# Two layers of a hybrid decoder on one core: recurrence outputs kept token-major, the forget gate inside a keys group, column groups interleaved in pairs

## The chip, the cores and the metric

The kernel runs on one core of a Trainium2 chip, as one launch. The metric is device time in microseconds (us), lower is better. Beside the timed runs there is one profiled execution, whose span is counted from its first to its last instruction. The engines are named as in the profile: PE is TensorE (matrix products), PEld its weight loads, DVE is VectorE, ACT is ScalarE, POOL is GpSimd, SP is SyncE, which here only issues DMAs.

## The reference, cut to what matters

256 tokens of width 2048 go through two layers. Every layer is a mixer and a gated MLP, each behind an RMS norm and added to the residual.

```python
# layer 0: mixer A (gMLP) and mixer B (HGRN2), 8 heads of 128 each
u, v, q, f, i, g = split(h @ w_in)
y_a = gelu(u) * (causal(sp_w) @ rms(gelu(v)) + sp_b)
k = (1 - lb) * sigmoid(-f);  decay = lb + (1 - lb) * sigmoid(f)
# state_t = decay_t * state_(t-1) + k_t v_t;  o_t = q_t state_t  (v is i here)
y_b = rms(o) * o_gain * silu(g)
x = x + concat(y_a, y_b) @ w_out
# layer 1: forgetting attention, 16 heads of 128
q, k, v, g, f = split(h @ w_in)           # f: 16 columns, one per head
c = cumsum(log_sigmoid(f + b_f))
p = softmax(rms(q) @ rms(k).T * scale + c[t] - c[s], causal)
x = x + ((p @ v) * sigmoid(g)) @ w_out
# both layers
z = conv3(h @ w_up);  x = x + (silu(z_a) * z_b) @ w_down
```

All weights and activations are float32.

## The kernel before, in words

The residual x lies feature-major, as 16 tiles of 128 features by 256 tokens (`xT`). A projection is made in groups of 512 output columns. Every float32 weight tile `w` comes from HBM by SP (L164), ACT rounds it to `wh` (L173), DVE subtracts to get the rest `wl` (L176), and PE sums three products of 128x512 for each of 16 k tiles and each of two token halves: high by high, high by low, low by high. That is 96 products in a group (`project_tok` L230 to L232; `project_four` L247 to L249, whose weights are four blocks of 128 columns). A step of the k loop brings two k tiles, so one `w` is 128x1024, half a megabyte; there are four buffers of `w` and three each of `wh` and `wl`, and six and five where `deep["pool"]` adds a second pool. The sums stand in PSUM banks of the pool `pm` (four banks, two for a group); everything small uses the four banks of `px`.

The group's result is token-major (tokens on partitions). Where the next step wants it feature-major, `transposed` (L252) turns it: two DVE block transposes (L255), then 16 DMAs of 32 KB, half of them issued by SP and half by POOL (L261).

Everything beside the main products is written as generators. `tick()` (L122), called once in every k step, admits generators from `queue` to `flight` up to `depth` and moves each on by one `yield`; so the position of a side step in program order is set by counting ticks. `LAG` ticks pass between the turning DMAs and their consumers, `WAIT` before the norm is finished. The framework then orders each engine's instructions by that program order and by its own estimate of when an instruction is ready; an order between two instructions can be added by hand (`add_manual_dep`).

Layer 0's mixer: two groups for v, then twice (j = 0, 1) the groups f, q, i of four heads, then two groups g, two groups u, four groups of the output projection (L707). The first group of the kernel is fed while x arrives (`feed`, `single`): its weights come in halves of 256 KB. For each head of mixer B, `hgrn` (L560) works feature-major on the tile `kq` with the second 128 tokens stored backwards: products of q and k on PE of which only the diagonal is kept (L568, L569), seven levels of masked scores (L599), a last cross product (L603), three products with the values `itok` (L620 to L622), whose second half was reversed before by a product with a permutation matrix (L662), a norm over the head, and two PE transposes (L635) back to feature-major with the gain (L638). `gated` (L672) multiplies that by silu(g) turned to feature-major, and `split` makes the high and low parts for the output projection, which takes mixer B's eight k tiles first (`names=ks`).

Layer 1's mixer: the first q group and the first k group (`early`, L723), `norm.finish()` (L726, a product L359 and a norm over tokens), the forget gate as a product group of its own (`forget` L734, through `project` L197 and L200: weights of 128 columns of which 16 count, result feature-major), then v and the other groups. q and k are normed and turned; `columns` (L751) transposes the summed gate; `attend` (L760) handles one head; `gate` (L843) multiplies by sigmoid(g) and turns; four groups of output projection.

The MLP (`ffn`, L881): `up` makes one group for each half of the gate, turns them (`tmp` has one buffer, `zt` two), convolves and multiplies; `down` sums over the hidden tiles. Groups run one after another everywhere: all 16 k tiles of one, then all 16 of the next.

Of the kernel before, what the change touches and what calls it, by code (L numbers as in the profile page):

```python
# [25 lines left out]
LAG = 4  # L26
WAIT = 4
EPS = 1e-6
WARM = 8
# [22 lines left out]
def tile_trunk(ctx: ExitStack, tc: tile.TileContext, x, pp_d, cst_d, mlev_d, msk_d,  # L52
# [30 lines left out]
    first_dma = nc.sync.dma_start(pp[:, 0:C_FFN], pp_d[:, 0:C_FFN])  # L83
# [24 lines left out]
    def back(ap):  # L108
        return view(ap, P - 1, (-1, P))

# [9 lines left out]
    flight, queue = [], []  # L120

    def tick():  # L122
        while queue and len(flight) < depth[0]:
            flight.append(queue.pop(0))
        for g in list(flight):
            if next(g, flight) is flight:
                flight.remove(g)
# [3 lines left out]
    def start(g):  # L131

        if next(g, g) is not g:
            flight.append(g)
# [5 lines left out]
    def drain():  # L140
        while flight or queue:
            tick()

    deep = {"pool": None, "turn": 0, "dma": first_dma}

    def in_order(r):
        tc.add_manual_dep(r.ins, deep["dma"].ins.name, order, reason="queue order")
        deep["dma"] = r


    def weights(src, n, rows=None, single=None):
# [17 lines left out]
        for i, p in enumerate(parts):  # L169
            if single:  # L170
                norm, k = single
                norm.feed_split(k + i, SC if k + i else V)
            deep["act"] = SC.activation(wh[:, p], w[:, p], AF.Copy)  # L173
            if deep["turn"] == 5:
                deep["hold"] = deep["act"]
            V.tensor_tensor(wl[:, p], w[:, p], wh[:, p].bitcast(F32), ALU.subtract)  # L176
        return wh, wl

    def project(wsrc, acts, chunks=(8, 8), k0=0, run=2, narrow=False):
# [3 lines left out]
        for c in chunks:  # L183
# [3 lines left out]
            for k1 in range(0, c, run):  # L187
# [11 lines left out]
                for k in ks:  # L199
                    PE.matmul(ps[:, S:2 * S], wl[:, k * P:(k + 1) * P], acts[done + k][:, 0:S],  # L200
                              start=False, stop=done + k == nk - 1, skip_group_check=True)
# [3 lines left out]
    def project_tok(wsrc, norm, feed=False):  # L205
        ps = [pm.tile([P, 512], F32, tag="pm", name=nm("pm")) for _ in range(2)]
        k = 0
        for c in (2,) * 8:
            if feed and k >= 8:
                for i in range(c):  # L210
                    norm.feed_split(k + i)
            tick()
            wh, wl = weights(wsrc[:, k * 512:(k + c) * 512], c * 512, single=(norm, k) if feed and k < 8 else None)
            if feed and k in BEHIND:
                in_order(nc.sync.dma_start(*fetch[BEHIND[k]]))
            if feed and k < 8:
                for i in range(c):
                    a = norm.a[k + i]
                    for j, (o, t) in enumerate(((0, wh), (S, wh), (0, wl))):
                        for T in range(2):  # L220
                            PE.matmul(ps[T], a[:, o + T * P:o + (T + 1) * P], t[:, i * 512:(i + 1) * 512],  # L221
# [3 lines left out]
            for T in range(2):  # L225
                for i in range(c):
# [5 lines left out]
                    PE.matmul(ps[T], al, h, start=False, stop=k + i == KT - 1)  # L232
# [3 lines left out]
    def project_four(w4, acts, n, k0=0, names=None):  # L236
        ps = [pm.tile([P, 512], F32, tag="pm", name=nm("pm")) for _ in range(2)]
        for k in range(0, n, 2):
            tick()
            lo = (k0 + k) * P  # L240
            wh, wl = weights(w4[:, :, lo:lo + 2 * P].rearrange("m p c -> p m c"), 1024, 4)
            for T in range(2):
                for i in range(2):
                    a = acts[names[k + i] if names else k + i]
# [4 lines left out]
                    deep['mm'] = PE.matmul(ps[T], al, h, start=False, stop=k + i == n - 1)  # L249
        return ps  # L250

# [13 lines left out]
    def fold(ps):  # L265
        t = tp.tile([P, S], F32, tag="ev", name=nm("ev"), bufs=3)
        SC.activation(t, ps[:, S:2 * S], AF.Copy)
        V.tensor_tensor(t, ps[:, 0:S], t, ALU.add)
        return t

    def project_norm(wsrc, acts, R, out=None, run=2):
        t = fold(project(wsrc, acts, run=run))
        if out is None:
            out = t
        V.tensor_tensor(out, t, R, ALU.mult)
        return out

    def split(dst, src, gain=None, eng=SC, turn=False):
        if turn:
            h, lo = (dst[:, i * S:(i + 1) * S].rearrange("p (t n) -> p t n", t=2) for i in range(2))  # L280
            src = turned(src)
            SC.activation(h, src, AF.Copy, scale=1.0 if gain is None else gain)
            if gain is None:
                V.tensor_tensor(lo, src, h.bitcast(F32), ALU.subtract)
            else:
                V.scalar_tensor_tensor(lo, src, gain, h.bitcast(F32), ALU.mult, ALU.subtract)
        elif gain is None:
            SC.activation(dst[:, 0:S], src, AF.Copy)
            V.tensor_tensor(dst[:, S:2 * S], src, dst[:, 0:S].bitcast(F32), ALU.subtract)
        else:  # L290
            if eng is SC:
                SC.activation(dst[:, 0:S], src, AF.Copy, scale=gain)
            else:
                V.tensor_scalar(dst[:, 0:S], src, gain, None, ALU.mult)
            V.scalar_tensor_tensor(dst[:, S:2 * S], src, gain, dst[:, 0:S].bitcast(F32),
                                   ALU.mult, ALU.subtract)

# [16 lines left out]
    class Norm:  # L314
# [8 lines left out]
        def feed_split(self, k, eng=SC):  # L323
            a = apool.tile([P, 512], F32R, tag="a", name=nm("a"), bufs=KT)
            split(a, xT[k], pp[:, self.col + k:self.col + k + 1], eng, self.turn)
            self.a[k] = a

# [12 lines left out]
        def feed(self, k):  # L340
            self.feed_split(k)
# [15 lines left out]
        def finish(self, tok=False):  # L357
            ps = bank()
            PE.matmul(ps[:, 0:S], ones, self.acc, start=True, stop=True)  # L359
            R = cp.tile([P, S], F32, tag="R", name=nm("R"), bufs=2)  # L360
            rsq(R, ps[:, 0:S], D)
            if not tok:
                return R
            for _ in self.finish_tok():
                pass
            return R, self.Rt

    def add_x(m, ps):
        t = tp.tile([P, S], F32, tag="ev", name=nm("ev"), bufs=3)
        SC.activation(t, ps[:, S:2 * S], AF.Copy)  # L370
        V.tensor_tensor(xT[m], xT[m], ps[:, 0:S], ALU.add)
        V.tensor_tensor(xT[m], xT[m], t, ALU.add)

    def add_four(q, ps, z, tmp, dst, nxt):
# [4 lines left out]
        def rest():  # L379
            for _ in range(LAG - (q == 3)):  # L380
                yield
# [742 lines left out]
```

## Time and profile before

| | us |
|---|---|
| median of 3 runs (lowest to highest) | 2308.27 (2307.07 to 2308.67) |
| the profiled execution | 2308.18 |
| its span | 2306.1 |
| PE busy, of the span | 2297.3 |
| DVE busy | 1559.2 |
| ACT busy | 1306.3 |
| POOL busy | 346.4 |

Matmuls are pipelined in the trace: each is shown for 0.39 us, but the next one starts long before its end, so the duration of a matmul group is read from starts, not from busy times. In the timeline a row is: start, duration, engine, line, operation, output<-inputs, shape, count, and in brackets the idle time before it and what ended it. In the chain of work that ended last a row is: start, duration, what.

### The profile page before, as it was taken

The numbers are of one execution on the slowest core, as the hardware profiler recorded it, in microseconds if no ns is written. First come the engines' busy times: TensorE is split into PE (matmuls) and PEld (weight loads), VectorE is DVE, ScalarE is ACT, GpSimd is POOL, SyncE is SP. The second block draws the span as 40 slices with busy tenths as digits, with TensorE's granted clock in tenths as the row PEclk, the third lists the DMA queues.
The fourth block names the chain that finished last, engine by engine and source line by source line (L and its number), as shares of the span: only waits on it lengthen the run. The fifth ranks groups of instructions, "written<-read, shape, count | busy, mean of one in ns | idle before, by whom it ended". The sixth has DMA issues, their size and how long they took to land.

```text
span 2306.1 us, 31359 instructions
## 1 busy us (share of the span) xinstructions
PE 2297.3 (100%) x10352; PEld 1902.7 (83%) x10352; DVE 1559.2 (68%) x2347; ACT 1306.3 (57%) x1960; POOL 346.4 (15%) x643
## 2 busy tenths in 40 slices
PE   9999999999999999999999999999999999999999
PEld 7888888888888888888888888888888888888887
DVE  7677866766567656765866665666776476667666
ACT  7567655665555545654565555655655465456543
POOL 0100112122012002111111101121221021012102
PEclk9999999999999999999999999999999999999999
DMA  8655577877666767776666565777777676667765
GB/s 275 205 160 174 173 220 217 251 217 215 208 209 207 219 199 209 222 218 188 197 228 197 180 190 173 229 219 237 231 218 217 193 216 209 206 204 219 220 204 174
DMA packets 497651, 481.43 MB, mean 209 GB/s; under 512 B 116592, under 2 KB 467712, under 8 KB 497360
## 3 DMA queue, kind: packets, MB, share of 16 engines
q1 hardware_dynamic: 474624, 452.90, 63.0%
q0 software_dynamic: 20560, 23.03, 4.4%
q10 hardware_dynamic: 2304, 3.51, 0.5%
q8 instruction: 81, 1.33, 0.2%
q14 instruction: 82, 0.67, 0.1%
HBM read 435.24 MB, written 2.11 MB: 190 GB/s over the span
## 4 chain that ended last, share of the span: by engine, by line
PE 95%; ACT 1%; DVE 1%; DMA 1%; issue 1%; SPq 0%; POOL 0%; ACTq 0%; DVEq 0%
PE pm L248 26%; PE pm L249 26%; PE pm L247 26%; PE pm L231 4%; PE pm L232 4%; PE pm L230 4%; ACT wh L173 1%; PE pm L221 0%; PE px L599 0%; PE pm L197 0%; SPq L261 0%; DVE wl L176 0%; DMA zt<-tmp 0%; PE px L768 0%; DMA turn<-tmp 0%
## 5 line engine op out<-in xcount | busy, mean ns | idle before, releaser
L176 DVE TENSOR_TENSOR wl<-w,wh 128x1024 fp32r<-128x1024 f32 (+1 forms) x822 | 998.2, 1218 | 645.2 <-ACT wh L173 637.0
L173 ACT ACTIVATE wh<-w 128x1024 fp32r<-128x1024 f32 (+1 forms) x822 | 863.5, 1054 | 788.9 <-PE pm L249 572.2
L248 PE MATMUL pm<-wl,a 128*128 128x512 f32 x1792 | 698.5, 390 | 0.8 <-DVE wl L176 0.8
L247 PE MATMUL pm<-wh,a 128*128 128x512 f32 x1792 | 698.9, 390 | 0.0
L249 PE MATMUL pm<-wh,a 128*128 128x512 f32 x1792 | 697.8, 389 | 0.0
L261 POOL DMA_DIRECT2D zt<-tmp x413 | 223.6, 549 | 1202.1 <-DVE tmp L255 1081.0
L248 PEld LDWEIGHTS pm<-wl,a 128*128 128x128 f32 x1792 | 336.6, 188 | 71.4 <-DVE wl L176 2.2
L249 PEld LDWEIGHTS pm<-wh,a 128*128 128x128 f32 x1792 | 336.5, 188 | 69.5
L247 PEld LDWEIGHTS pm<-wh,a 128*128 128x128 f32 x1792 | 336.5, 188 | 69.3 <-ACT wh L173 0.3
L248 PE MATMUL pm<-wl,hid 128*128 128x512 f32 x688 | 267.8, 389 | 0.3 <-DVE wl L176 0.3
L247 PE MATMUL pm<-wh,hid 128*128 128x512 f32 x688 | 267.6, 389 | 0.0
L249 PE MATMUL pm<-wh,hid 128*128 128x512 f32 x688 | 267.6, 389 | 0.0
L261 POOL DMA_DIRECT2D turn<-tmp x224 | 121.5, 550 | 741.1 <-DVE tmp L255 336.3
L230 PE MATMUL pm<-wh,a 128*128 128x512 f32 x496 | 195.7, 395 | 0.0
L231 PE MATMUL pm<-wl,a 128*128 128x512 f32 x496 | 193.5, 390 | 1.4 <-DVE wl L176 1.3
L232 PE MATMUL pm<-wh,a 128*128 128x512 f32 x496 | 193.3, 390 | 0.0
L248 PEld LDWEIGHTS pm<-wl,hid 128*128 128x128 f32 x688 | 129.1, 188 | 27.6 <-DVE wl L176 0.7
L247 PEld LDWEIGHTS pm<-wh,hid 128*128 128x128 f32 x688 | 129.1, 188 | 26.8
L249 PEld LDWEIGHTS pm<-wh,hid 128*128 128x128 f32 x688 | 129.1, 188 | 26.7
L231 PEld LDWEIGHTS pm<-wl,a 128*128 128x128 f32 x496 | 93.2, 188 | 21.4 <-DVE wl L176 2.6
L916 ACT ACTIVATE conv<-zt,pp 128x256 f32<-128x256 f32 x176 | 95.4, 589 | 25.3 <-DMA zt<-tmp 18.5
L232 PEld LDWEIGHTS pm<-wh,a 128*128 128x128 f32 x496 | 93.2, 188 | 19.4
(213 smaller groups left out, 1833.9 us busy)
## 6 DMA issues: line engine op xcount, KB each, us to landing
w<-in_w_up SPq DMA_DIRECT2D x352, 512.0 KB, 4.5
w<-in_w_dn SPq DMA_DIRECT2D x176, 512.0 KB, 4.5
w<-in_w_cqkv SPq DMA_DIRECT2D x96, 512.0 KB, 4.3
w<-in_w_abo SPq DMA_DIRECT2D x32, 512.0 KB, 4.7
w<-in_w_cg SPq DMA_DIRECT2D x32, 512.0 KB, 4.2
w<-in_w_co SPq DMA_DIRECT2D x32, 512.0 KB, 4.7
zt<-tmp SPq DMA_DIRECT2D x414, 32.0 KB, 2.8
zt<-tmp POOLq DMA_DIRECT2D x413, 32.0 KB, 2.6
```

Source lines behind the costliest of these rows:

```text
L173: deep["act"] = SC.activation(wh[:, p], w[:, p], AF.Copy)
L176: V.tensor_tensor(wl[:, p], w[:, p], wh[:, p].bitcast(F32), ALU.subtract)
L230: PE.matmul(ps[T], ah, h, start=k + i == 0, stop=False)
L231: PE.matmul(ps[T], ah, l, start=False, stop=False)
L232: PE.matmul(ps[T], al, h, start=False, stop=k + i == KT - 1)
L247: PE.matmul(ps[T], ah, h, start=k + i == 0, stop=False)
L248: PE.matmul(ps[T], ah, l, start=False, stop=False)
L249: deep['mm'] = PE.matmul(ps[T], al, h, start=False, stop=k + i == n - 1)
L261: qs[(a + b) % len(qs)].dma_start(dst[BLK * b:BLK * (b + 1), :, a * n:(a + 1) * n], tmp[BLK * a:BLK * (a + 1), b * 4 * n:(b + 1) * 4 * n] ...
L916: SC.activation(c, z, AF.Identity, bias=pp[:, cb:cb + 1], scale=w(2))
```

## The change

- **Recurrence.** The second 128 tokens are no longer stored backwards and the values no longer reversed. The diagonal of q k is no longer taken from a PE product: after the f group one ACT and one DVE instruction form the keys token-major for four heads (`of_keys`), and after the q group eight DVE multiply-and-accumulate instructions give the diagonal (`of_queries`). One PE transpose of the second half's scores is new. The normed output is written token-major into `itok` and is not transposed back; `gated` multiplies token-major, then turns by the DMAs, and applies the gain in the split. The groups u now run before the groups g, and the output projection takes mixer A's k tiles first (`shift`).
- **Forget gate.** Its 16 weight columns lie beside the 512 of the first keys group (`keys_gate`): one k tile at a time, 528 columns wide, the 16 columns loaded by POOL and the 512 by SP, each of the 96 products replaced by one of 272 and one of 256 columns. `norm.finish()` goes. The gate is turned by four small PE transposes.
- **Interleaving.** The first two groups of mixer outputs, of both MLPs and of layer 1's mixer run as: 12 k tiles of the first, 12 of the second, 4 of the first, 4 of the second.
- **Ties.** `LAG` 4 to 6 (7 for a stage's last group), `WAIT` 4 to 2; consumers of turned pieces start from a list counted in ticks (`after`) and are ordered by hand behind the last weight rounding, subtraction or main product (`behind`). q and k are normed and turned by a generator.
- **Start.** The first parameters are loaded by ACT's queue, between the first two pieces of x, not by SP ahead of the weights; the first roundings on ACT are ordered by hand (`"first"`); 7 warm-up products, not 8.

```diff
-LAG = 4
-WAIT = 4
+LAG = 6
+LAST = 7
+WAIT = 2
+JOIN = 12
-WARM = 8
+WARM = 7
     SC.dma_start(*fetch[0])
-    first_dma = nc.sync.dma_start(pp[:, 0:C_FFN], pp_d[:, 0:C_FFN])
+    SC.dma_start(pp[:, 0:C_FFN], pp_d[:, 0:C_FFN])
     SC.dma_start(*fetch[1])
...
+    def after(n, g):
+        soon.append([n, g])
+    def behind(r, what):
+        if what in deep:
+            tc.add_manual_dep(r.ins, deep[what].ins.name, order, reason="behind what was handed over")
+        return r
...
+    def project_pair(wa, wb, acts, shift=0):
+        pa, pb = banks_for(), banks_for()
+        for part in ((0, JOIN), (JOIN, KT)):
+            for w4, ps in ((wa, pa), (wb, pb)):
+                project_four(w4, acts, KT, shift=shift, ps=ps, part=part)
+                if part[1] == KT:
+                    yield ps
...
-            dg = bank()
-            for T in range(2):
-                PE.matmul(dg[:, T * P:(T + 1) * P], t[:, T], t[:, 3 - T], start=True, stop=True)
-            V.tensor_tensor(st, dg[:, 0:S].rearrange("p (a b) -> p a b", a=2),
-                            ident.unsqueeze(1).to_broadcast([P, 2, P]), ALU.mult)
+            V.tensor_tensor(st, ident.unsqueeze(1).to_broadcast([P, 2, P]),
+                            dgc[:, h].unsqueeze(2).to_broadcast([P, 2, P]), ALU.mult)
...
+            turn_in(op[:, S:S + P], st[:, 1], ident)
+            SC.activation(st[:, 1], op[:, S:S + P], AF.Copy)
...
-            tps = bank()
-            for T in range(2):
-                PE.transpose(tps[:, T * P:(T + 1) * P], ot[:, T], ident)
-            for T, src in enumerate((tps[:, 0:P], back(tps[:, P:S]))):
-                tt = slice(T * P, (T + 1) * P)
-                V.tensor_scalar(l[:, tt], src, pp[:, C_ON:C_ON + 1], None, ALU.mult)
...
-            ps = bank()
-            PE.matmul(ps, cst[:, K_REV:K_REV + P], itok[:, 1], start=True, stop=True)
-            SC.activation(itok[:, 1], ps, AF.Copy)
...
+        def keys_gate(part):
+            for k in range(*part):
+                if k % 2 == 0:
+                    tick()
+                w = wp.tile([P, n], F32, tag="w", name=nm("w"), bufs=4)
+                wh = wp.tile([P, n], F32R, tag="wh", name=nm("wh"), bufs=3)
+                wl = wp.tile([P, n], F32R, tag="wl", name=nm("wl"), bufs=3)
+                nc.gpsimd.dma_start(w[:, 0:CH], w_cf[:, k * P:k * P + CH])
+                nc.sync.dma_start(w[:, CH:n], w_cqkv[CH // 4][:, k * 512:(k + 1) * 512])
+                deep["act"] = SC.activation(wh, w, AF.Copy)
+                deep["sub"] = V.tensor_tensor(wl, w, wh.bitcast(F32), ALU.subtract)
...
+                        PE.matmul(pa[T][:, 0:CH + S], a_, t[:, 0:CH + S], start=begin, stop=end)
+                        deep["main"] = PE.matmul(pb[T][:, 0:S], a_, t[:, CH + S:n], start=begin, stop=end)
+        first = banks_for()
+        for part in ((0, JOIN), (JOIN, KT)):
+            project_tok(w_cqkv[0], norm, ps=first, part=part)
+            keys_gate(part)
...
-        R, Rt = norm.finish(), norm.Rt
+        Rt = norm.Rt
-            f = project_norm(w_cf, A, R, hp.tile([P, S], F32, tag="f", name="f"))
```

396 lines of the change are left out of this document (219 added, 177 removed).

## The prediction

> **What bounds the kernel now.** I read the page first, then PE's groups by form, then PE's timeline where its products stop being evenly spaced.
>
> ```profile
> span 2306.1 us, 31359 instructions
> ...
> PE 2297.3 (100%) x10352; PEld 1902.7 (83%) x10352; DVE 1559.2 (68%) x2347; ACT 1306.3 (57%) x1960; POOL 346.4 (15%) x643
> ...
> PE 95%; ACT 1%; DVE 1%; DMA 1%; issue 1%; SPq 0%; POOL 0%; ACTq 0%; DVEq 0%
> ```
>
> PE is on the chain of work that ended last for 95% of the span, and no other engine comes near. So there are only two ways to gain: fewer or shorter products on PE, and the few places where PE waits. What ACT, DVE, SP and POOL do counts only where it makes PE wait.
>
> The price of one product is read from starts. Here are the end of an ordinary group, the whole forget gate of before, and the next group:
>
> ```profile
> 1153.17 0.39 PE L232 MATMUL pm<-wh,a 128*128 128x512 f32 x1
> ...
> 1155.21 0.39 PE L232 MATMUL pm<-wh,a 128*128 128x512 f32 x1
> 1155.44 0.59 PE L359 MATMUL px<-acc,ones 128*128 128x256 f32 x2
> 1155.68 0.82 PE L197 MATMUL pm<-a,wh 128*128 128x512 f32 x2
> ...
> 1161.46 0.40 PE L230 MATMUL pm<-wh,a 128*128 128x512 f32 x1
> ```
>
> From 1153.17 to 1155.21 there are nine starts: 2.04 / 9 = 0.227 us for a 512-wide product. With two k tiles to a step, 12 products make 2.72 us. The 96 products of a group make 21.8 us.
>
> **The change, part by part.**
>
> *Forget gate.* What goes is the stretch from 1155.44 (the token norm L359) to 1161.46: **6.0 us**. What comes is the split of 96 products of 512 columns into 96 of 272 and 96 of 256. The nearest rows are 256-wide products that follow each other, at the very end of the kernel:
>
> ```profile
> 2302.04 0.40 PE L193 MATMUL pm<-hid,wh 128*128 128x256 f32 x2
> 2302.28 0.28 PE L193 MATMUL pm<-hid,wl 128*128 128x256 f32 x1
> ```
>
> Two starts in 0.24, so 0.120 us each. Between 256 columns (0.120) and 512 (0.227) a column is worth 0.42 ns, so 272 columns cost 0.127. The pair costs 0.247 against 0.227, 0.020 more, and 96 of them **1.9 us**. The ends: not below nothing, since there are more columns and more instructions; at most 0.120 more each, 11.5 us, if 272 columns cost as much as 512. I take 1.9, since 272 lies next to 256. The Trainium skill (TensorE: Matmul & The Clock Gate, Back-to-back issue gap) gives N/2.4 + 2.5 ns, by which the split would cost 225.0 instead of 215.8 ns, 0.9 us in all, and the forecast would be 1.0 us lower. The trace does not agree with it here: 227 and 120 ns stand where it has 216 and 109.
>
> *Recurrence.* The reversal of the values (L662) and the products for the diagonal (L568) go:
>
> ```profile
> 121.84 1.12 PE L662 MATMUL px<-itok,cst 128*128 128x512 f32 x2
> 122.80 1.50 PE L568 MATMUL px<-kq 128*128 128x128 f32 x12
> 124.06 0.48 PE L248 MATMUL pm<-wl,a 128*128 128x512 f32 x1
> ```
>
> ```profile
> L568 PE MATMUL px<-kq 128*128 128x128 f32 x32 | 4.3, 275 | 0.0
> L635 PE MATMUL px<-cst,ot 128*128 128x128 f32 x16 | 4.3, 308 | 0.2
> ```
>
> L662 takes 122.80 - 121.84 = 0.96 us and is made twice (j = 0, 1): 1.9. L568 takes 1.26 us for 12 records, 0.105 each, and has 32: 3.4. Together **5.3 us**. The transposes L635 go from two to one for each of eight heads:
>
> ```profile
> 166.22 0.56 PE L635 MATMUL px<-cst,ot 128*128 128x128 f32 x2
> 166.55 0.48 PE L248 MATMUL pm<-wl,a 128*128 128x512 f32 x1
> ```
>
> Two cost 0.33, so one less saves 0.165 and eight **1.3 us**. The gate's four small transposes take the place of the two of `columns`: 0.3 us more. PE's work thus falls by 6.0 - 1.9 + 5.3 + 1.3 - 0.3 = **10.4 us**.
>
> The diagonal moves to ACT and DVE (two wide instructions and eight short ones for each four heads), while the copies out of PSUM, half the gate sigmoids and the gain at the old place go. I cost this at nothing; the cover is:
>
> ```profile
> 120.00:280.00 160.00, 159.41 (x793) 130.13 (x792) 125.78 (x351) 109.44 (x281) 17.41 (x32) 1.00 0.54 166
> ```
>
> In the recurrence's stretch DVE (third figure) is busy 125.8 of 160 us and ACT 109.4. If that cover were gone, each short DVE instruction would push back a `wl` for which PE waits.
>
> *Ties and interleaving.* PE visibly waits for `wl` at three places, each time behind consumers of turned pieces on ACT and DVE:
>
> ```profile
> 1233.82 0.41 PE L230 MATMUL pm<-wh,a 128*128 128x512 f32 x1
> 1235.00 0.50 PE L231 MATMUL pm<-wl,a 128*128 128x512 f32 x1 [0.77 <-DVE wl L176]
> ```
>
> ```profile
> 1598.02 0.50 PE L247 MATMUL pm<-wh,a 128*128 128x512 f32 x1
> 1599.28 0.50 PE L248 MATMUL pm<-wl,a 128*128 128x512 f32 x1 [0.76 <-DVE wl L176]
> ```
>
> ```profile
> 1975.04 0.39 PE L247 MATMUL pm<-wh,hid 128*128 128x512 f32 x1
> 1975.74 0.50 PE L248 MATMUL pm<-wl,hid 128*128 128x512 f32 x1 [0.31 <-DVE wl L176]
> ```
>
> Taking 0.227 from each distance leaves 0.95, 1.03 and 0.47 us: 2.45 in all. That is everything the lags can give back; I take **2.0**. Interleaving gives 12 k tiles of a second group, 16 us, before the last pieces of the stage before are needed, but no further stall stands there to be removed.
>
> What the longer lag makes late: the gated pieces of the last four heads. Their chain (gate, turn, seven ticks of 2.72 us, about 20 us) ends before the output pair asks for them, after 24 k tiles or 33 us. That is covered.
>
> *The keys group's own feed.* It goes by one k tile, so four `w` buffers hold half of what they held, and each k tile waits for a POOL DMA as well, 16 in place of none (SP loses the gate's two loads). POOL's queue also carries half the turning DMAs, but those of the stage before were issued 16 us earlier. On ACT a rounding that waits for its loads has the residual's splits and squares queued behind it (L292, L333), and the norm waits for those. The ties by hand (`behind`) only order instructions on one engine. PE needs a new tile every 6 x 0.247 = 1.48 us. The supply:
>
> ```profile
> DMA to landing us min/median/max: 3.3/4.5/9.5
> ```
>
> ```profile
> L173 ACT ACTIVATE wh<-w 128x512 fp32r<-128x512 f32 x8 | 4.7, 624 | 1.3 <-DMA w<-in_w_v 1.3
> ```
>
> ```profile
> L176 DVE TENSOR_TENSOR wl<-w,wh 128x512 fp32r<-128x512 f32 x8 | 5.3, 690 | 1.2 <-ACT wh L173 1.2
> ```
>
> ```profile
> zt<-tmp POOLq DMA_DIRECT2D x413, 32.0 KB, 2.6
> ```
>
> A buffer's round is landing + 0.62 + 0.69: by the median 5.8 us, by the least 4.6 us, shared by four buffers 1.45 or 1.15 us a tile. POOL's small load lands sooner (2.6). It is just enough, nearer to enough as these loads have half the bytes of the median's. The residual sums and splits of the stage before fall into the same stretch on ACT and DVE; for them, and for a turn that meets another, I allow **1.5 us** of new waits.
>
> *Start.*
>
> ```profile
> 0.74 0.42 ACTq L82
> 1.19 3.52 DMA x<-in_x
> 4.80 0.51 ACT a L292
> 5.30 0.53 ACT wh L173
> 5.88 11.23 PE pm L221 x48
> ```
>
> Before, the first rounding of weights stands on ACT behind the split of the second piece of x. The order by hand puts it ahead, which takes 0.51 us off this chain, and SP's first weight load moves from 1.19 to 0.74, a further 0.45. So the gain is up to 0.95. It may all be lost when the later weight halves, which are not faster, become the limit; and moving the parameters to ACT's queue delays the second x by one issue, up to 0.45 worse. I take **0.5**.
>
> ```profile
> 1.06 3.78 PE L138 MATMUL warm<-ones 128*128 128x128 f32 x16 [1.06 <-DVE one L86]
> ```
>
> The warm-up records stand 0.21 apart (3.6 us for 16), twice the 0.105 of the same shape in L568. The Trainium skill (TensorE: Matmul & The Clock Gate, Part 1) has the array at half clock until about 3.4 us of sustained work; by that, one warm-up product less and an earlier start could leave up to 3.4 us of main products at half speed, which would lose 1.7 us and make the forecast 2.2 us higher without the start's gain. The trace agrees on the half speed, and by 5.88 on its end.
>
> **The sum.** -10.4 - 2.0 - 0.5 + 1.5 = **-11.4 us**. The profiled execution took 2308.18 us (span 2306.1 and 2.1 around it), 0.09 from the median of 2308.27, so nothing is corrected: 2308.18 - 11.4 = **2296.8**. Without new waits and with all of the start and the stalls it is -13.8; waits ahead of the recurrence's bursts that also vanish could add three or four.
>
> **The rivals.**
>
> 1. *The lags give nothing.* The three stalls and the start stay, because other work takes the place of what was moved: -10.4 + 1.5, 2299.3. For it: each stall ends with DVE, which gets no less work. Against it: the stalls stand where turned pieces are consumed, and those move. Chance 0.10.
> 2. *Two turns meet in the MLPs.* The two first groups now end 24 products, 5.4 us, apart, and `tmp` has one buffer.
>
> ```profile
> 1583.27 5.11 SPq L261 DMA_DIRECT2D turn<-tmp  x8
> ```
>
> Eight issues and a landing (2.6) make 7.7 us, so the second transpose is 2.3 us early. If it stands in DVE's queue ahead of `wl`, that waits too; PE's three `wl` buffers (8.2 us) speak against it. Twice 2.3 makes 2301.4. Chance 0.06.
> 3. *The keys group is fed too slowly in part.* With a landing of 6.5 us a tile takes 1.95 us, 0.47 too long, and 16 tiles lose 7.5: 2304.3. Chance 0.10.
> 4. **The other side:** *the keys group starves outright.* If the paired loads of SP and POOL land as late as the worst of before, 9.5 us, a tile takes 2.70 us, 1.22 too long, 19.6 us in all: 2316.4. It decides from where the round eats the 11.4 us gained: 0.71 us a tile, a round of 8.8 us, a landing of 7.5. Against it: the median of twice the bytes is 4.5. Chance 0.04.
>
> **How the numbers follow.** The forecast has 0.70, with 2292 to 2300 as its own stretch. From 2290 to 2302 it holds the forecast and rivals 1 and 2, 0.86. About 0.2%, 4.6 us, is what a measurement here tells from no change, so faster means under 2303.7: 0.70 + 0.10 + 0.06 and some 0.04 of rival 3 make 0.90, the same 0.06, slower 0.04.
>
> **What would show it.** The gate's stretch gone and 272-wide starts 0.127 apart from the next; no L662 or L568 kind of product; no distance over 0.5 us before a `wl` product in the attention or at an MLP; the first main product near 5.0 us. Wrong would be: tiles of the keys group more than 1.6 us apart, DVE held by a block transpose early in an MLP, or main products of the first 3 us twice as long.

## The result, and the profile after

The changed kernel takes **2315.24 us** (median of 7 runs, 2314.13 to 2317.44) where the kernel before takes 2308.27 (median of 7 runs, 2306.47 to 2308.95). The ratio is 1.0033, 95% interval 1.0021 to 1.0045: slower by about 7 us. Forecast were 2296.8, 11 us faster. Both the sign and the range were wrong. The profiled execution took 2317.44 us with a span of 2315.7, which is 9.6 more than the span of before. It is the slowest of the seven, 2.2 us above their median, so the trace shows a somewhat larger loss than the median does.

From the page of the changed kernel: the span; busy times; the chain that ended last by engine; and, from the groups, the products whose idle time stands out (busy time, mean ns, then idle time before them and what ended it).

```profile
span 2315.7 us, 31427 instructions
...
PE 2292.7 (99%) x10370; PEld 1903.9 (82%) x10370; DVE 1557.9 (67%) x2369; ACT 1313.3 (57%) x1953; POOL 356.5 (15%) x661
...
PE 75%; DMA 2%; DVE 1%; SPq 1%; issue 0%; ACT 0%; DVEq 0%; ACTq 0%; POOLq 0%
...
L267 PE MATMUL pm<-wh,a 128*128 128x512 f32 x464 | 184.3, 398 | 8.3 <-ACT wh L206 8.3
```

DMA (2%) and SP's queue (SPq 1%) now stand on the chain, and one line of products has 8.3 us of idle time. The timeline of PE shows that this is a single wait, near the start of the attention:

```profile
1181.17 0.39 PE L269 MATMUL pm<-wh,a 128*128 128x512 f32 x1
1189.83 1.22 PE L267 MATMUL pm<-wh,a 128*128 128x512 f32 x2 [8.27 <-ACT wh L206]
```

Two things must be kept apart: what PE has to do, and how long it waits. I took the distance from each PE start to the next over the whole span, and from it the price of that shape (0.227 us for 512 columns). What is left over sums to 22.5 us before and 42.5 us after: **20.0 us more waiting**. PE's last product ends 8.8 us later (2302.56 before, 2311.35 after), so its work fell by 20.0 - 8.8 = **11.2 us**. The tail behind the last product grew from 3.5 to 4.3 us. -11.2 + 20.0 + 0.8 = +9.6, the difference of the spans. The change does what it was priced to do on PE, and loses twice as much in waits that were not there.

Where the new waiting lies, by the same sums in stretches of 50 us: 12.2 us at the attention (1150 to 1200: 1.1 before, 13.3 after), 5.0 at the output of layer 0's mixer (350 to 400), 3.3 at that of layer 1's (1550 to 1600: 1.1 and 4.4) and 0.9 at the first MLP (450 to 500). About 1.8 more stand between 50 and 100 (0.9 and 2.7), of which 1.07 is one wait for DVE's `wl` at 51.2; between 100 and 350 about 3 us of waiting are gone. SP's timeline around the largest (a row groups issues of one kind; a stretch of 16 is two turns):

```profile
1159.91 6.08 SPq L195 DMA_DIRECT2D w<-in_w_cqkv  x3
1168.65 16.12 SPq L314 DMA_DIRECT2D turn<-tmp  x16
1184.87 6.52 SPq L195 DMA_DIRECT2D w<-in_w_cqkv  x5
```

For 16.1 us SP issues nothing but turning DMAs, and from its last weight load (issued by 1165.99) to the next one 18.9 us pass. The weights of the next group stand behind them in the same queue; the last before them was issued at 1165.66, and PE ran dry at 1181.4. POOL's timeline shows what else went on:

```profile
1166.92 0.56 POOL L807 DMA_DIRECT2D cb<-cd  x1 [2.02 <-DMA cd<-fc]
1168.88 3.82 POOL L314 DMA_DIRECT2D turn<-tmp  x7 [1.40 <-DVE ss L350]
1178.08 4.89 POOL L314 DMA_DIRECT2D turn<-tmp  x9 [5.38 <-DMA turn<-tmp]
```

`cb<-cd` is the broadcast of the summed forget gate to all partitions, 128x4096 float32, 2 MB. It lands 10.9 us after its issue, the turns are issued just behind it, and both POOL and SP stop until a turn has landed. The chain that ended last passes exactly here:

```profile
1169.29 11.01 DMA turn<-tmp
1180.32 0.58 SPq L314
...
1184.87 3.76 DMA w<-in_w_cqkv
...
1188.72 1.06 ACT wh L206
1189.83 1.22 PE pm L267 x2
```

One turning DMA of 32 KB takes 11.01 us; a like one takes 2.4 in the median (page: `zt<-tmp SPq`). Before, the same work lay apart. SP's timeline of the kernel before:

```profile
1151.32 6.05 SPq L261 DMA_DIRECT2D turn<-tmp  x8
1157.48 3.97 SPq L164 DMA_DIRECT2D w<-in_w_cqkv  x4
1164.48 5.12 SPq L261 DMA_DIRECT2D turn<-tmp  x8
1169.72 26.22 SPq L164 DMA_DIRECT2D w<-in_w_cqkv  x12
```

The q turn and the k turn were 13 us apart with four weight loads between them, and the broadcast came behind both, at 1176.28. That q turn was issued at 1151.32, before the k group's last product at 1155.21. The changed kernel starts the q turn only after the keys group, whose last product starts at 1156.00, and issues it at 1168.65, so the two turns and the broadcast meet.

The wait has a second price. In a table by stretches of PE (length, busy time and count of PE, PEld, DVE, ACT, POOL, then the granted clock, DMA share, GB/s):

```profile
1180.00:1189.80 9.80, 1.55 (x7) 0.94 (x5) 0.00 (x0) 1.99 (x3) 2.97 (x6) 0.82 0.63 180
1189.80:1196.00 6.20, 6.14 (x16) 4.58 (x17) 5.25 (x9) 2.96 (x4) 0.00 (x0) 0.50 0.87 305
1196.00:1200.00 4.00, 4.00 (x18) 3.27 (x17) 2.28 (x7) 2.46 (x7) 0.00 (x0) 0.94 0.34 128
```

For some 6 us after the wait the granted clock is 0.50, and products of 512 columns start 0.43 apart: about 3.5 us more are lost. The other two places look the same on a smaller scale. SP and PE at the two mixer outputs:

```profile
338.19 11.80 SPq L314 DMA_DIRECT2D turn<-tmp  x16
350.10 8.07 SPq L195 DMA_DIRECT2D w<-in_w_abo  x6
```

```profile
355.10 0.73 PE L287 MATMUL pm<-wh,yb 128*128 128x512 f32 x2 [1.99 <-ACT wh L206]
```

```profile
1540.46 11.16 SPq L314 DMA_DIRECT2D turn<-tmp  x16
1551.73 8.39 SPq L195 DMA_DIRECT2D w<-in_w_co  x6
```

```profile
1556.73 0.73 PE L287 MATMUL pm<-wh,yc 128*128 128x512 f32 x2 [1.35 <-ACT wh L206]
```

There is no broadcast here, and SP is held for the bare 16 issues, 11 to 12 us.

### The profile page after: what moved, and what is told of

It reads as the page before. It is cut to its first block, busy times and chain, and to the rows that moved or that the text cites. A ratio compares the mean times of both kernels' runs of the same rounds, so it can differ in the third digit from the quotient of the medians.

```text
span 2315.7 us, 31427 instructions
## 1 busy us (share of the span) xinstructions
PE 2292.7 (99%) x10370; PEld 1903.9 (82%) x10370; DVE 1557.9 (67%) x2369; ACT 1313.3 (57%) x1953; POOL 356.5 (15%) x661
## 4 chain that ended last, share of the span: by engine, by line
PE 75%; DMA 2%; DVE 1%; SPq 1%; issue 0%; ACT 0%; DVEq 0%; ACTq 0%; POOLq 0%
PE pm L288 21%; PE pm L289 21%; PE pm L287 21%; PE pm L267 3%; PE pm L268 3%; PE pm L269 3%; SPq L314 1%; DMA zt<-tmp 1%; PE px L161 1%; PE px L770 1%; DMA turn<-tmp 0%; PE pm L771 0%; DVE wl L211 0%; DVE tmp L308 0%; PE px L164 0%
## 5 line engine op out<-in xcount | busy, mean ns | idle before, releaser
L211 DVE TENSOR_TENSOR wl<-w,wh 128x1024 fp32r<-128x1024 f32 (+1 forms) x812 | 986.7, 1218 | 655.6 <-ACT wh L206 650.0
L206 ACT ACTIVATE wh<-w 128x1024 fp32r<-128x1024 f32 (+1 forms) x812 | 854.6, 1054 | 796.3 <-PE pm L289 555.6
L288 PE MATMUL pm<-wl,a 128*128 128x512 f32 x1792 | 698.4, 390 | 2.9 <-DVE wl L211 2.9
L287 PE MATMUL pm<-wh,a 128*128 128x512 f32 x1792 | 701.0, 391 | 0.0
L289 PE MATMUL pm<-wh,a 128*128 128x512 f32 x1792 | 698.1, 390 | 0.0
L288 PEld LDWEIGHTS pm<-wl,a 128*128 128x128 f32 x1792 | 336.8, 188 | 73.3 <-DVE wl L211 4.6
L267 PE MATMUL pm<-wh,a 128*128 128x512 f32 x464 | 184.3, 398 | 8.3 <-ACT wh L206 8.3
L268 PE MATMUL pm<-wl,a 128*128 128x512 f32 x464 | 181.9, 392 | 0.2 <-DVE wl L211 0.2
L269 PE MATMUL pm<-wh,a 128*128 128x512 f32 x464 | 181.6, 391 | 0.0
L308 DVE STREAM_TRANSPOSE tmp<-z 128x512 f32<-128x512 f32 x132 | 92.2, 706 | 18.4 <-ACT z L974 16.0
```

Source lines behind the costliest of these rows:

```text
L211: deep["sub"] = V.tensor_tensor(wl[:, p], w[:, p], wh[:, p].bitcast(F32), ALU.subtract)
L267: PE.matmul(ps[T], ah, h, start=k + i == 0, stop=False)
L268: PE.matmul(ps[T], ah, l, start=False, stop=False)
L269: deep["main"] = PE.matmul(ps[T], al, h, start=False, stop=k + i == KT - 1)
L287: PE.matmul(ps[T], ah, h, start=k + i == 0, stop=False)
L288: PE.matmul(ps[T], ah, l, start=False, stop=False)
```

## The experiments

**Theory A:** two turns that follow each other too closely hold SP's in-order queue, the weights behind them come late, PE runs dry, and its clock is halved on top; the broadcast makes it worse. **Theory B:** the cost lies in the longer lags, ties and open groups on ACT and DVE. **Theory C:** the bytes of the broadcast alone. All edits are to the changed kernel. The kernel before had medians of 2308.1 to 2308.6 beside these runs.

### Turns apart at the outputs

The four groups of an output one after another again (with two gated pieces to a tick, so that they are ready in time):

```diff
     def output(w, acts, shift=0):
-        yield from project_pair(w[0:4], w[4:8], acts, shift)
-        for q in (2, 3):
+        for q in range(4):
...
-                yield
+                if i % 2:
+                    yield
```

> The changed kernel, but the two output projections run their four groups one after another (no interleaved pair there; the last gated pieces of layer 1 are made two to a tick so that they come in time). Theory A: the stalls at the output projections (2.2 + 0.7 and 1.5 + 0.7 us and the half-clock stretches behind them, about 9 us in all) go, the one of 8.4 us in the attention stays, time 2304 to 2308. Theories B and C: 2313 to 2317.

Measured: 2307.16 us (2305.79 to 2309.17), ratio to before 0.9995 [0.9986, 1.0005]. The waits at 352 and 1555 are gone, that of the attention stays (7.2 us idle). As A has it, 8 us better than the changed kernel.

This leaves open whether interleaving costs as such or only brings two turns together. One number tells:

```diff
-JOIN = 12
+JOIN = 8
```

> The changed kernel with one number altered: JOIN 8 in place of 12, so that two interleaved groups end 48 products, 10.9 us, apart and not 24 products, 5.4 us. Two turns on SP (5.1 us each) then no longer follow each other without a gap at the outputs and in the MLPs; in the attention the q turn starts only after the keys group, so there they still meet. Theory A (it is the distance of the two turns against the 5.1 us that each holds SP): the waits at 352, 462 and 1555 with their half-speed products go (5.0, 1.0 and 3.2 us), SP issues no run of 16 turning DMAs there, the attention's wait of 7 to 9 us stays, and the time is 2304 to 2309. If interleaving as such costs (more open groups, later sums on ACT and DVE), these waits stay or move, and the time is 2311 to 2317.

Measured: 2308.42 us (2303.44 to 2310.74), 0.9998 [0.9989, 1.0007]. SP's timeline at the output of layer 0's mixer, and at the attention:

```profile
336.58 1.63 SPq L195 DMA_DIRECT2D w<-in_w_abo  x3
342.25 5.11 SPq L314 DMA_DIRECT2D turn<-tmp  x8
347.46 11.46 SPq L195 DMA_DIRECT2D w<-in_w_abo  x7
```

```profile
1162.80 18.00 SPq L314 DMA_DIRECT2D turn<-tmp  x16
```

Weights now stand between the turns. The sums of the waits fall from 5.0 to 0.4 us in 350 to 400, from 0.9 to nothing in 450 to 500 and from 4.4 to nothing in 1550 to 1600, with the groups still interleaved. The attention, where the q turn waits for the keys group whatever JOIN is, still loses its wait (10.2 us idle). So it is the **distance of the two turns**, not interleaving.

### The attention: two turns and a broadcast

All turning DMAs on POOL, none on SP:

```diff
-                qs = queues or (nc.sync, nc.gpsimd)
+                qs = queues or (nc.gpsimd,)
```

> The changed kernel, but all 16 DMAs of every turn are issued by POOL, none by SP (the last turn of the kernel keeps its three queues). Theory A (two turns that meet hold SP's queue, the weight loads stand behind them, PE runs dry and its clock is halved for a while): the stalls of 8.4, 2.2 and 1.5 us and the slow products behind them go, about 12 + 5 + 4 us, time 2293 to 2298. Theory B (the stalls come from the longer lag and the ties on ACT and DVE): no change, 2314 to 2317. Theory C (the bytes of the gate's broadcast alone starve the weights): the stall of 8.4 us stays at over 6, 2313 or more.

Measured: 2321.99 us (2318.41 to 2323.06), 1.0057 [1.0042, 1.0072], so the time missed A's range. By its number alone it falls into theory C's (2313 or more), but C's sign, a wait of over 6 us in the attention, is absent. What A said of the waits did come true: PE's last product ends at 2305.0, 6.4 us earlier than in the changed kernel, and the waits at 352, 1181 and 1555 are gone. But POOL has become the held queue. It carries the gate's 16 columns for the keys group, and its timeline and PE's show these behind turns:

```profile
1109.79 8.66 POOL L314 DMA_DIRECT2D zt<-tmp  x16 [8.42 <-DVE tmp L308]
1118.44 2.42 POOL L761 DMA_DIRECT2D w<-in_w_cf  x4
```

```profile
1122.50 0.58 PE L770 MATMUL px<-wh,a 128*128 128x272 f32 x1 [2.99 <-ACT wh L763]
```

And at the kernel's end, where the last turns stand behind each other in POOL's queue, the span ends 16.3 us after the last product, not 4.3.

The next edits take the suspects one by one. First the broadcast left out:

```diff
+            V.memset(cb, 0.0)
...
-            nc.gpsimd.dma_start(cb, cd.partition_broadcast(P))
```

> The changed kernel without the gate's broadcast: the per-key gate sums are zeros, so a term of the attention scores is left out. Theory A (the meeting turns hold SP's queue, and the broadcast only makes them last longer): the turns land in 2 to 3 us again and the stall of 8.4 us in the attention falls to 1 to 3 us, since the turns still meet; time 2305 to 2310. Theory C (the broadcast's bytes alone): the stall falls under 0.5 us and the clock stays whole there, 2302 to 2305. Theory B (lags and ties): 2314 to 2317.

Measured: 2312.57 us (2310.5 to 2315.38), 1.002 [1.0011, 1.003], above A's range and in none of the others. Turns land in 1.9 to 3.7 us, SP is held for 11.2 us and not 16.1, and three waits of 0.8, 1.5 and 1.4 us remain: the stall shrinks as A has it, and does not vanish as C has it. Part of the time is the edit's own: its `memset` holds DVE for 3.47 us at 1135.88, and PE waits 1.09 us behind it, outside the stretch that is compared below.

Then only the second of two meeting turns on POOL alone (attention, outputs and MLPs), with the broadcast in its place:

```diff
+    POOLED = (nc.gpsimd,)
...
-        transposed(lambda T: z[:, T], tmp, dst)
+        transposed(lambda T: z[:, T], tmp, dst, POOLED if q == 1 else None)
...
-                    start(turn(z, t))
+                    start(turn(z, t, POOLED if ps is None else None))
...
-            zb, eb = four(HT + j0, pair and next(pair))
+            zb, eb = four(HT + j0, pair and next(pair), POOLED if pair else None)
```

> The changed kernel, but of two turns that meet (first two groups of the outputs and of both MLPs, first q and k) the second is issued by POOL alone; every other turn keeps both queues. Theory A: SP is held for 5 us instead of 11; the stalls at both outputs and in the first MLP go, and the tail is as short as before; in the attention at most 2 us are left. 2293 to 2299. Theory B: 2314 to 2317. Theory C: the stall in the attention stays over 6 us, 2304 to 2307.

Measured: 2304.8 us (2303.7 to 2308.02), 0.9986 [0.9977, 0.9995]. That is 10 us better than the changed kernel, but above A's range (2293 to 2299) and within the time of C's (2304 to 2307). The attention still waits 4.15 us, more than A's 2 and less than C's 6, and runs at half clock behind it. SP's timeline shows what is left:

```profile
1163.09 7.51 SPq L314 DMA_DIRECT2D turn<-tmp  x8
1174.91 16.66 SPq L195 DMA_DIRECT2D w<-in_w_cqkv  x9
```

SP has only one turn, but its eight DMAs fly beside the broadcast, and SP issues the next weights only when the first of the eight has landed, at 1174.84.

Then both turns on SP and POOL as changed, but the broadcast tied behind POOL's half of them:

```diff
+                if q_ is nc.gpsimd:
+                    deep["turned"] = r
...
-            nc.gpsimd.dma_start(cb, cd.partition_broadcast(P))
+            for _ in range(5):
+                yield
+            behind(nc.gpsimd.dma_start(cb, cd.partition_broadcast(P)), "turned")
```

> The changed kernel with the broadcast kept but tied on POOL's queue behind the turns of the first q and k; the ticks of the run with the late broadcast had not moved it. Theory A: stall of 1 to 3 us at the turns, and weight loads beside the broadcast land late but from a full ring, as before the change; 2305 to 2311. Theory C: the stall comes later, at the broadcast, with over 5 us; 2313 or more.

Measured: 2314.82 us (2312.26 to 2316.7), 1.0026 [1.0015, 1.0037]. That misses A's range, and both the time and the wait are what was expected of theory C, a later stall of over 5 us. The trace shows how it comes about. Most turns land within 4.0 us, but they still hold SP for 11.0 us, so that SP's last three turning DMAs and the weights issued behind them at 1180.82 now fly beside the broadcast (1178.59 to 1186.58). The three land at 1186.8 to 1187.1, the first weights at 1188.13. The wait is 5.3 us; it ends with a product that needs the last turned piece, and the weights would not have been there sooner. Moving the broadcast alone moves the loss from the first turns to the last ones and the weights.

Both edits together:

> The second of two meeting turns on POOL alone and the broadcast tied behind them. Theory A: no stall over 1.5 us from the first output projection on and the clock whole, 2292 to 2297. Theory C: as with the broadcast tied behind, its stall comes later, 2300 or more.

Measured: **2299.54 us** (2299.0 to 2302.11), 0.9965 [0.9952, 0.9978], faster than both kernels, though 2.5 us above A's range (2292 to 2297), and a wait of 1.90 us is left at the second output, where A had none over 1.5. SP's timeline:

```profile
1162.80 5.10 SPq L315 DMA_DIRECT2D turn<-tmp  x8
1168.01 23.35 SPq L195 DMA_DIRECT2D w<-in_w_cqkv  x11
```

The stretch from 1150 to 1200 in four kernels, in one fence each: as changed; broadcast left out; second turn on POOL; second turn on POOL and the broadcast behind (same columns as above, PE's busy time first, its clock third from the end).

```profile
1150.00:1200.00 50.00, 41.69 (x194) 34.12 (x193) 30.96 (x53) 23.75 (x41) 9.78 (x18) 0.90 0.72 221
```

```profile
1150.00:1200.00 50.00, 46.93 (x229) 38.45 (x228) 33.63 (x57) 29.20 (x53) 9.24 (x17) 0.97 0.67 207
```

```profile
1150.00:1200.00 50.00, 45.39 (x194) 36.17 (x193) 31.13 (x51) 24.57 (x40) 14.13 (x26) 0.93 0.80 240
```

```profile
1150.00:1200.00 50.00, 49.74 (x233) 40.26 (x232) 36.00 (x60) 29.69 (x55) 14.10 (x26) 1.00 0.79 259
```

By the sums of waits this is 13.3, 6.9, 8.7 and 2.7 us, with 1.1 before. Leaving out the broadcast gives 6.4, the second turn on POOL 4.6, the tied broadcast by itself (9.6 us of waits) about 3.5, the second turn on POOL with the tied broadcast 10.6. Neither alone is the cause. Theory C falls, since waits remain without the broadcast and nearly all go with it kept; A holds with two holders of the queue.

Two further kernels tell little. The broadcast five ticks later in program order, without a tie:

```diff
+            for _ in range(5):
+                yield
             nc.gpsimd.dma_start(cb, cd.partition_broadcast(P))
```

> The changed kernel, but the broadcast of the summed forget gate to all partitions (2 MB) is issued five ticks later, behind the turns of the first q and k. Theory A: the turns land in 2 to 3 us again, but they still meet, so a stall of 2 to 3 us stays in place of 8.4, time 2306 to 2310. Theory B: 2314 to 2317. Theory C: the stall goes or moves with the broadcast; if it goes 2303 to 2305, if it moves no change.

Measured: 2315.7 us (2313.2 to 2319.65), 1.0032 [1.0022, 1.0043]. The framework still issued the broadcast ahead of the turns (at 1167.96), so the edit did not do what it was for, and the run decides nothing. The same holds for it joined with all turns on POOL:

> All turns on POOL and the broadcast five ticks later. Theory A: as with the turns on POOL alone or up to 2 us better, 2292 to 2297, no stall over 1.5 us in the attention. Theory B: 2314 to 2317. Theory C: 2303 to 2306.

Measured: 2324.53 us (2321.3 to 2326.85), 1.007 [1.0055, 1.0085].

### Lags and interleaving by themselves

The best kernel so far with the lags of before:

```diff
-LAG = 6
-LAST = 7
-WAIT = 2
+LAG = 4
+LAST = 3
+WAIT = 4
```

> The run that measured 2299.5, with the lags alone put back: LAG 4, LAST 3, WAIT 4 in place of 6, 7 and 2; interleaving, ties and everything else stay. If the lags are what took away the three waits for DVE of the kernel before (0.95, 1.03 and 0.47 us, at the starts of the attention and the MLPs), these come back, with the clock still whole, and the time is 2301 to 2303. If interleaving or the ties took them away, or other work stands there, the time stays within 2298.5 to 2300.5.

Measured: 2301.78 us (2299.72 to 2303.19), 0.9972 [0.996, 0.9983]. The median lies in the range that was expected if the lags had taken the waits away, but the interval overlaps that of 2299.54, so the time does not decide. The trace, which is of the fastest of the six runs (2299.72), speaks against the lags. Three stretches that hold the places of the old waits at 1233, 1598 and 1975:

```profile
1200.00:1440.00 240.00, 240.00 (x1135) 200.81 (x1134) 154.61 (x239) 138.40 (x242) 30.27 (x56) 1.00 0.61 188
1570.00:1640.00 70.00, 70.00 (x312) 58.05 (x311) 45.80 (x59) 40.99 (x55) 17.32 (x32) 1.00 0.82 252
1940.00:2000.00 60.00, 60.00 (x266) 49.71 (x265) 37.38 (x46) 28.05 (x33) 4.33 (x8) 1.00 0.69 210
```

PE is busy for the whole of all three. The waits did not come back in this execution, so it was not the lags alone that took them away. Ties and interleaving were both still in; the next kernel has the ties without the interleaving.

No interleaving anywhere, with the lags of before, which groups in turn need:

```diff
-LAG = 6
-LAST = 7
-WAIT = 2
+LAG = 4
+LAST = 3
+WAIT = 4
...
-        first = banks_for()
-        for part in ((0, JOIN), (JOIN, KT)):
-            project_tok(w_cqkv[0], norm, ps=first, part=part)
-            keys_gate(part)
+        first = project_tok(w_cqkv[0], norm)
...
+                    keys_gate((0, KT))
                     start(forget())
...
-            pair = project_pair(w_up[l, 0:4], w_up[l, HT:HT + 4], A) if j0 == 0 else None
+            pair = None
```

(and the outputs in turn as above)

> The changed kernel with no groups interleaved anywhere (outputs, MLPs, the attention's q and keys groups in turn) and the lags of before (4, 3, 4), which the groups in turn need; recurrence, the gate's columns in the keys group, ties, start and the broadcast stay as changed; no turn is put on POOL alone. Theory A: turns stand 20 us apart, the waits at 352, 462 and 1555 go, only the broadcast is left beside one turn; PE's saved 11.2 us and the start's 0.4 remain, less up to 6 us for the broadcast and up to 2.5 us for the three waits for DVE that may come back: 2297 to 2304. Theory B: the keys group's own feed (a POOL load for each tile, 528 columns wide) is what runs dry, so a wait of 7 us or more stays between 1150 and 1200 and the time is 2305 or more.

Measured: 2311.24 us (2307.44 to 2312.98), 1.001 [1.0001, 1.0019]: by its number on the side of what is called theory B there, the keys group's own feed, though the wait of 6.09 us stands earlier than expected. The q turn now falls into the middle of the keys group. SP and PE:

```profile
1139.87 5.10 SPq L313 DMA_DIRECT2D turn<-tmp  x8
1145.08 1.99 SPq L761 DMA_DIRECT2D w<-in_w_cqkv  x4
```

```profile
1152.17 0.60 PE L769 MATMUL px<-wh,a 128*128 128x272 f32 x1 [6.09 <-ACT wh L762]
```

This group's buffers hold one k tile each, 1.48 us of work, and each tile comes through SP and POOL; a single turn of 5.1 us is enough to empty them. What came last were POOL's 16 columns: the 512 of the tile that PE waited for landed at 1148.26, the 16 at 1151.31, because POOL issued them only behind its own half of the turn, at 1147.27. When the keys group was undisturbed (the changed kernel) it ran evenly. So the same mechanism, a turn ahead of weights in a queue, starves the group that has least in store. The broadcast beside the k turn cost another 3.3 us of idle time at 1189.5.

The trace also answers what the lags left open. The same three stretches as above:

```profile
1200.00:1440.00 240.00, 240.00 (x1144) 201.30 (x1143) 154.21 (x239) 136.87 (x241) 27.08 (x51) 1.00 0.61 185
1570.00:1640.00 70.00, 70.00 (x312) 58.03 (x311) 49.88 (x70) 42.20 (x61) 15.22 (x29) 1.00 0.79 237
1940.00:2000.00 60.00, 60.00 (x266) 49.71 (x265) 39.26 (x52) 31.36 (x41) 7.64 (x15) 1.00 0.73 218
```

With the lags of before and nothing interleaved, the three old waits are still gone. So neither the lags nor the interleaving took them away; the ties are the likeliest cause that is left, and they were not taken out by themselves.

### Best versions

Turns apart at the outputs on top of the second turn on POOL and the tied broadcast:

> The second of two turns that meet goes by POOL alone and the broadcast is tied behind it (as in the run that measured 2299.5), and the four output groups of each mixer follow one another again. Theory A (turns that meet hold SP's in-order queue): the last turns that still meet, those of the outputs, are apart, the wait of 2.06 us near 1551 goes, no product of the output stages waits over 0.7 us, and the time is 2296 to 2298.5. Theory B (interleaving two groups covers some other wait, and the cost lies in ACT and DVE): waits come back at the start of the outputs or of the MLPs behind them, and the time is 2300 or more.

Measured: 2300.99 us (2299.45 to 2302.03), 0.9968 [0.9956, 0.998], outside A's range and in the time of theory B's (2300 or more). The wait near 1551 is gone as expected, but one near 1461 that the best kernel also has (0.62 and 0.76 us idle) grew to 1.54 and 0.76 and was followed by half-speed products. What makes that wait was not tried. In this trace ACT takes four turned pieces (`yc`, from 1459.46, when the last turning DMA had landed at 1459.24) ahead of the rounding that PE waits for, at 1461.67: a small cost of theory B's kind.

JOIN 8 with those two repairs in the attention alone:

> JOIN 8 as in the run before it, and in the attention alone the second turn on POOL and the broadcast tied behind it. Theory A: no two turns meet on SP anywhere, so what is left of the waits is the attention's 1 to 3 us, and the time is 2296 to 2300, at or below the 2299.5 of the best run so far. If interleaving as such costs, or turns on POOL were what saved the outputs and the MLPs, waits of 2 us or more come back at 352, 462 or 1551 and the time is 2302 or more.

Measured: 2299.0 us (2297.49 to 2303.73), 0.9965 [0.9953, 0.9978]. With no two turns meeting on SP, 16.2 of the changed kernel's 2315.24 us come back. Its trace is of the slowest of the five runs (2303.73), and there the attention still waits 2.0 us. This and 2299.54 cannot be told apart.

## Why the prediction was wrong

- **PE's work: right.** Forecast -10.4 us, measured -11.2. The keys group's starts, from its timeline:

```profile
1128.79 0.29 PE L770 MATMUL px<-wh,a 128*128 128x272 f32 x1
1128.92 0.28 PE L771 MATMUL pm<-wh,a 128*128 128x256 f32 x1
...
1131.75 0.29 PE L770 MATMUL px<-wh,a 128*128 128x272 f32 x1
```

  Twelve pairs from 1128.79 to 1131.75 make 0.247 us a pair, as forecast, and 0.13 for the first of them. The gate's stretch, the diagonal and the reversal are gone.
- **Start: forecast -0.5, no gain shown.** The 61st main product starts at 20.79 where before it was 20.78, the 193rd at 51.22 against 51.66: 0.4 earlier. But the wait at 51.2 follows at once, and the 194th starts at 52.51 against 51.89. In the traces of the thirteen other kernels with this start the 193rd comes between 50.14 and 53.83, at 51.8 in the median. The picture was wrong too: the first product comes at 5.73, not near 5.0, since the parameters now land later on ACT's queue and DVE's first `a` waits for them; the first products start 0.43 apart, which is half speed by their distance although the granted clock stands at 1.00 there. The prediction had named this as a sign against it (the sentence drawn from the Trainium skill, TensorE: Matmul & The Clock Gate, Part 1, allowed for it). The 13th main product comes at 9.91 instead of 8.77; what is made up after that comes mainly from two waits of before, at 17 and 21 us, that are gone.
- **Stalls, -2.0: right in place, wrong in cause.** All three are gone in the changed kernel, but they stay gone with the lags of before, and with these lags and no interleaving as well.
- **New waits, +1.5: this is the step that failed.** In its place stand about 21 us at four places: 12.2, 5.0, 3.3 and 0.9 (the 1.8 between 50 and 100 wait for DVE and are another matter). The working weighed the turns of the stage before against the keys group, and asked of two meeting turns only whether they share `tmp`. It had the row with SP's eight issues, 5.11 us, and read it as the turn's own delay, not as 5.1 us in which no weight is issued. Two of them make over 11 us of silence in the one queue that feeds PE, more than the buffers of weights cover at these places.
- **The part by part left out what a moved step issues.** The gate's broadcast was never counted: 2 MB, which before landed behind both turns and now flies beside them. With it SP is held 16.1 us; without it 11.2.
- **Clock.** That a wait would be followed by products at half speed was priced nowhere. After the wait of 8.27 us it cost about 3.5 us, and at the outputs 1.5 to 2 each.
- **"No further stall stands there to be removed", of interleaving.** True, but it was priced only as a gain of nothing; it also moves the ends of two groups to 5.4 us from each other.
- **The rivals.** Rival 2 had the right event, two turns that meet, the wrong resource and a price of 4.6 us. Rivals 3 and 4 did not occur in the changed kernel, where the group runs at its 1.48 us a tile; their condition appears only when a turn is put into that group, as in the kernel without interleaving. Rival 4's time, 2316.4, is near the measured one by chance, not by its mechanism.

The repaired kernels, at 2299.0 and 2299.5, lie 2 to 3 us above the forecast. Where the queue is free, the largest term, PE's work, shows in the time; that the end comes so near is in part luck, since the start gave nothing and small waits are left.

## What to carry to other kernels

Where one in-order queue issues both the weights and other transfers, count for every moved step how long its issues occupy that queue, and compare the longest run without a weight load with what the weight buffers hold. When two groups are interleaved, the distance of their ends must exceed the time that their follow-up work holds a queue by enough for weight loads to go between: 5.4 us against 5.1 did not do here, 10.9 did. A wait of PE should be priced with the slow products behind it, and a large transfer with what the small ones beside it wait for.

## What the runs showed of the hardware

- Small transfers beside a large one: the first turning DMAs of 32 KB behind the 2 MB broadcast landed after 7 to 11 us, and without it they took 1.9 to 3.7.
- Issuing stops at a certain number of unlanded transfers, as it seems eight: POOL issued the broadcast and seven turns and then sat idle for 5.38 us until one had landed. In none of the fifteen traces had SP or POOL more than eight transfers that were issued and not landed.
- Moving turns to POOL helped although the bytes stayed the same. The Trainium skill (Trainium Kernel Development and Optimization, Key Constraints) says that DMAs from SP, ACT and POOL run on the same 16 DMA engines and that issuing from several saves only issue time; here that issue time, 5.1 us a turn, is what counted where no broadcast was near, and the trace agrees. Beside the broadcast SP also stood still until transfers had landed, so that one turn on SP held back the weights until 1174.91 in the kernel with the second turn on POOL.
- The clock fell after a wait as short as 1.35 us with another of 0.53 close behind it, while a single wait of 1.90 us did not lower it. From the timeline of the best kernel, and its clock there:

```profile
1553.68 0.50 PE L288 MATMUL pm<-wl,yc 128*128 128x512 f32 x1 [1.90 <-DVE wl L211]
```

```profile
1550.00:1560.00 10.00, 8.10 (x36) 6.33 (x35) 9.28 (x16) 7.60 (x14) 4.33 (x8) 1.00 0.38 98
```

  The Trainium skill (TensorE: Matmul & The Clock Gate, Part 1) gives an idle window of about 3.4 us for the fall; the half-speed stretches here last 3.4 us or a multiple (3.4, 10.2 and 3.4 by the clock's own records), but shorter waits than that window set them off.
